# Gate stage of a PEER block: two-byte compares, scaling and copies swapped between engines, 64 early expert rows, and a new share of side work per step

## The chip, the cores and the metric

The kernel runs on one core of a Trainium2 chip. Its time is the device time of one execution in microseconds (us), the median of several. The engines are called PE (TensorE, matmuls), PEld (its weight loads), DVE (VectorE), ACT (ScalarE), POOL (GpSimd) and SP (SyncE, which here only issues DMAs). Every engine works through its own instructions in order.

## The reference, cut to what matters

Two transformer blocks over 512 tokens of width 1024, all in float32. The change lies in the first block, in the part called PEER: every token picks, for each of 8 heads, 16 experts out of 128 x 128, and adds their value vectors, weighted.

```python
q = (nf @ w_q).reshape(t, PEER_HEADS, D_KEY)
s1 = jnp.einsum("thd,hkd->thk", q1, sub_keys[:, 0])
s2 = jnp.einsum("thd,hkd->thk", q2, sub_keys[:, 1])
v1, i1 = lax.top_k(s1, TOPK)
v2, i2 = lax.top_k(s2, TOPK)
cand = (v1[..., :, None] + v2[..., None, :]).reshape(t, PEER_HEADS, TOPK * TOPK)
vals, ci = lax.top_k(cand, TOPK)
e1 = jnp.take_along_axis(i1, ci // TOPK, axis=-1)
e2 = jnp.take_along_axis(i2, ci % TOPK, axis=-1)
idx = (e1 * N_KEYS + e2).reshape(t, PEER_HEADS * TOPK)
gates = jax.nn.softmax(vals.astype(jnp.float32), axis=-1).astype(n.dtype)
# for each block of 128 tokens:
act = jax.nn.gelu(jnp.einsum("td,tkd->tk", xb, expert_u[ib])) * gb
out = jnp.einsum("tk,tkd->td", act, expert_v[ib])
```

After it the second block begins with a state space mixer, whose tables (powers of the transition, input and output maps) depend on weights alone.

## The kernel before, in words

Every weight arrives as a strip of 128 x 1024 numbers (`wr`, loaded by SP), is split in two halves whose sum it is (`wh` by ACT, line 148; `wl` by DVE or POOL, line 150), and is multiplied in three matmuls (lines 161 to 163). Two strips ahead are split, four ahead are loaded (`next_strip`).

Tokens 128 to 511 are done **densely**, for all experts: the scores of 128 groups of 128 experts (strips `exp_u`) are computed, multiplied by a table `gd` that holds each token's gate for each expert and zero elsewhere, and multiplied by the value strips (`exp_v`) into six PSUM banks `pv` (line 1143). Tokens 0 to 127 are done by **rows**: for each of 128 slots a gather (POOL, line 1009) brings the u and v vectors of the expert that each token picked; DVE forms the dot product (line 1012) and adds the weighted v vector (line 1043).

The work falls in three stretches. First come the 16 query strips, with the top-16 picks on DVE. Then the **gate stage** (`plan_gates`): PE works on the u strips of 64 expert groups, whose results go out to memory (`sd`), and beside it a list `bg` of background items is worked off. An item has a cost, and after each strip items are taken until the strip's share of the total cost is used (`run_bg`). The items are:

- the choice of experts for a block of 128 tokens (`plan_choice`): candidates, top 16, and per head a look-up `look(h)`, in which DVE compares (line 861), POOL multiplies (line 864) and DVE reduces two heads later (line 868); then `ints` turns numbers to integers, `trans` transposes them on PE and copies them with ACT to the tables `e1T`, `e2T`, `gT`.
- 48 fronts of 8 tokens: `front(i)` builds one-hot tables, `oh2` (line 917, all 8 tokens, float32), `oh1` (line 925, four tokens, bf16 out) and `gh`, the one-hot times the gate, with ACT from `oh1` for four tokens (line 929) and with DVE in one step for the other four (line 931); `mid(i)` multiplies them on PE into two PSUM tiles `pg` (line 941); `back(i)` copies these with ACT to `gb` (line 948), from which ACT issues stores to `gd`. The number table they are compared with, `iotaP` (in the tile `held`), lies in PSUM as float32.
- `EARLY` = 32 row dots, each with a gather of the u half alone: 12 among the second block's 16 fronts, 12 among the third's, 8 after all else (`TAIL`).

Then the **dense stage** (`dense`): 128 steps, each with 18 `pv` matmuls and, in 64 of them, the 24 matmuls of a u strip not done before. How much background follows each step is set by `rates`. The background list is the rows (a cost of 1.2 for a slot whose dot is already done, 2.4 for one that needs gather, dot, gate and add) with the state space prep (`ssm_prep`: about 20 chains on DVE, then 16 parts of small POOL products, a few PE products, and stores that ACT issues) spread between them in proportion to cost. SP loads, in order, strips, the saved scores `gs` and every fourth step a 768 KB piece `G` of `gd`, four steps ahead of its use.

Of the kernel before, what the change touches and what calls it, by code (L numbers as in the profile page):

```python
# [36 lines left out]
class K:  # L37
# [557 lines left out]
    EARLY = 32  # L595
# [6 lines left out]
    NV = 4  # L602
    CV = 4
# [40 lines left out]
    def peer(self):  # L644
# [16 lines left out]
        iotaP = self.bank("mmc", (P, P), "held")  # L661
# [10 lines left out]
        self.bg = [(0.1, lambda: nc.scalar.copy(iotaP, iota))] + bias  # L672
# [63 lines left out]
        for what, i in self.q_order()[2:]:  # L736
            if what == "q":
                self.lin(xq, p_q(i))
            else:
                self.lin(nr, p_s(i), w=TD)  # L740
                done += 1
            if (what, i) == ("q", 11):
                self.run_bg(1000)
                part = self.plan_choice(vals, idx, iotaP, st_["rc"])
                self.bg += part(1, 0)
                self.bg_rate, self.credit = sum(c for c, _ in self.bg) / 8, 0
# [7 lines left out]
        self.plan_gates(part, iota, iotaP, gd, early)  # L754
# [49 lines left out]
    def plan_choice(self, vals, idx, iota, rc):  # L804
# [5 lines left out]
        self.eT = e1T, e2T, gT = [loc((P, TD), tag=t) for t in ("e1T", "e2T", "gT")]  # L810
        state = {}

        def part(b, half):
# [4 lines left out]
            def cands():  # L818
                if not half:
                    d["c"], d["k"] = loc((P, 8, NCD), tag="cand"), loc((P, 8, NCD), tag="code")  # L820
                    d["v"] = loc((P, 8, 16), tag="cv")
                    d["i"] = loc((P, 8, 16), U16, tag="ci")
                    d["e"] = loc((P, 8, 16), tag="ee")
# [32 lines left out]
            sh = [P, 16, NCD]  # L856

            def look(h):
                if h < 4 * half + 4:
                    eq = loc((P, 16, NCD), tag="eq", bufs=1 + self.LG)  # L860
                    nc.vector.tensor_tensor(
                        eq, d["i"][:, h, :].unsqueeze(2).to_broadcast(sh), iota[:, 0:NCD].unsqueeze(1).to_broadcast(sh), ALU.is_equal
                    )
                    nc.gpsimd.tensor_tensor(eq, eq, d["k"][:, h, :].unsqueeze(1).to_broadcast(sh), ALU.mult)
                    d["eq", h] = eq
                h -= self.LG
                if h >= 4 * half:
                    nc.vector.tensor_reduce(d["e"][:, h, :], d["eq", h], AX.X, ALU.add)

            if half:  # L870
                items += [(0.3, soft)]
# [16 lines left out]
            def trans():  # L888
                pt = self.px_((P, 3, P), "pt")
                nc.tensor.transpose(pt[:, 0, :], d["ef"][:, 0, :], self.ident)  # L890
                nc.tensor.transpose(pt[:, 1, :], d["ef"][:, 1, :], self.ident)
                nc.tensor.transpose(pt[:, 2, :], d["g"].rearrange("p a b -> p (a b)"), self.ident)
                o = slice(b * P - P, b * P)
                for j, t in enumerate((e1T, e2T, gT)):
                    nc.scalar.copy(t[:, o], pt[:, j, :])

            return items + [(self.IC if b == 1 else 0.8, ints)] + ([(0.3, trans)] if b else [])
# [3 lines left out]
    def plan_gates(self, part, iota, iotaP, gd, step):  # L901
# [3 lines left out]
        A = HT - self.NV  # L905
# [7 lines left out]
        def front(i):  # L913
            t0 = i * HT
            sh = [P, HT, P]
            oh2 = self.loc((P, HT, P), tag="oh2", bufs=2)
            nc.vector.tensor_tensor(
                oh2, e2T[:, t0 : t0 + HT].unsqueeze(2).to_broadcast(sh), iotaP.unsqueeze(1).to_broadcast(sh), ALU.is_equal
            )
            gh = self.loc((P, HT, P), tag="gh", bufs=2)  # L920
            A = HT - self.NV
            if A:
                oh1 = self.loc((P, A, P), BF16, tag="oh1", bufs=2)
                sh1 = [P, A, P]
                nc.vector.tensor_tensor(oh1, e1T[:, t0 : t0 + A].unsqueeze(2).to_broadcast(sh1), iotaP.unsqueeze(1).to_broadcast(sh1), ALU.is_equal)
# [38 lines left out]
        turn = {0: part(1, 1), 1: nxt[1], 2: nxt[2]}  # L964
        turn = {b: (x, x.pop())[1] for b, x in turn.items()}
        bg = part(1, 1)[:-1] + nxt[1][:3] + [turn[0]]
        nxt[1] = nxt[1][3:]
# [3 lines left out]
        for b in range(1, NB):  # L971
# [7 lines left out]
            for j in range(k):  # L979
                i = b * k - k + j  # L980
                bg.append((self.FC, lambda i=i: front(i)))
                if i >= 1:
# [82 lines left out]
    def dense(self, nr, gd, sd, xd, step):  # L1065
# [15 lines left out]
        costs, at, to = sum(c for c, _ in items), 0.0, 0  # L1081
        for it in items:
            at += it[0]
# [8 lines left out]
        scale = total / sum(rates[:-4])  # L1092
        rates = [r * scale for r in rates]

        def load(e):
            if e >= P:
                return
            if e % GG == 0:
                t = self.loc((P, NC, GG, TC), tag="G", bufs=2)
                nc.sync.dma_start(t, gd[:, :, e : e + GG, :].rearrange("c p e t -> p c e t"))  # L1100
                G[e // GG] = t
            if e in ahead:
# [18 lines left out]
        def unit_u(e):  # L1121
            load(e + 4)
            if e in ahead:
# [5 lines left out]
        self.bg_rate = 0  # L1129
        for e in range(4):  # L1130
            load(e)
        for e in range(L):
            unit_u(e)
        for e in range(P):
# [92 lines left out]
    def ssm_prep(self):  # L1227
# [144 lines left out]
        def part(q):  # L1372
# [29 lines left out]
            def w2(r):  # L1402
# [3 lines left out]
                w, x = self.loc(sh2, tag=f"w2{r}"), self.loc(sh2, tag="w2x")  # L1406
# [5 lines left out]
            def wc(r):  # L1412
# [3 lines left out]
                w, x = self.loc(sh3, tag=f"wc{r}"), self.loc(sh3, tag="wcx")  # L1416
# [798 lines left out]
```

## Time and profile before

| | us |
|---|---|
| median of 3 executions (3007.21 to 3015.2) | 3007.63 |
| the profiled execution, its own time | 3011.37 |
| its span in the trace | 3009.6 |
| gate stage, from the start of the one-hot work to the last early strip | 349 to 697 |
| dense stage, `pv` matmuls | 711 to 1591 |

The profiled execution is 3.7 us above the median, and 1.8 us of its time lie outside the span. PE is busy for 2870.4 us. [...] To read the profile: for each stretch take PE's idle time and lost clock, which is all that a change beside PE can give back, and look which engine PE waited for.

### The profile page before, as it was taken

The numbers are of one execution on the slowest core, as the hardware profiler recorded it, in microseconds if no ns is written. First come the engines' busy times: TensorE is split into PE (matmuls) and PEld (weight loads), VectorE is DVE, ScalarE is ACT, GpSimd is POOL, SyncE is SP. The second block draws the span as 40 slices with busy tenths as digits, with TensorE's granted clock in tenths as the row PEclk, the third lists the DMA queues.
The fourth block names the chain that finished last, engine by engine and source line by source line (L and its number), as shares of the span: only waits on it lengthen the run. The fifth ranks groups of instructions, "written<-read, shape, count | busy, mean of one in ns | idle before, by whom it ended". The sixth has DMA issues, their size and how long they took to land. (4 is left out here: it accounts for less than half of the span.)

```text
span 3009.6 us, 39311 instructions
## 1 busy us (share of the span) xinstructions
PE 2870.4 (95%) x14286; PEld 2428.0 (81%) x14286; DVE 2168.8 (72%) x3783; ACT 1257.4 (42%) x2200; POOL 1111.8 (37%) x937
## 2 busy tenths in 40 slices
PE   8999999998999999999999989999999998999998
PEld 6787999998888788877877768888878766888886
DVE  7849888986889888888876764766566366566665
ACT  4443355664334333333335443333344355433333
POOL 3134776752268787788762311000011011100001
PEclk9999999999999999999999999999999999999999
DMA  4236446788889899988873653332332211233323
GB/s 143 63 108 144 162 160 223 248 298 286 281 300 344 305 335 332 328 311 325 323 253 134 173 184 91 92 93 89 100 110 84 64 53 53 89 101 98 98 71 98
DMA packets 237793, 537.92 MB, mean 179 GB/s; under 512 B 35802, under 2 KB 130410, under 8 KB 224928
## 3 DMA queue, kind: packets, MB, share of 16 engines
q1 hardware_dynamic: 172896, 346.84, 35.2%
q0 software_dynamic: 25232, 140.74, 13.2%
q10 hardware_dynamic: 39472, 47.84, 4.5%
q8 instruction: 113, 1.85, 0.3%
q14 instruction: 80, 0.66, 0.1%
HBM read 470.33 MB, written 65.01 MB: 178 GB/s over the span
## 5 line engine op out<-in xcount | busy, mean ns | idle before, releaser
L150 DVE TENSOR_TENSOR wl<-wr,wh 128x1024 fp32r<-128x1024 f32 (+2 forms) x445 | 539.2, 1222 | 501.6 <-ACT wh L148 498.0
L148 ACT ACTIVATE wh<-wr 128x1024 fp32r<-128x1024 f32 (+2 forms) x552 | 545.2, 995 | 430.8 <-PE mm L163 220.5
L161 PE MATMUL mm<-xn,wh 128*128 128x512 f32 x1296 | 515.5, 398 | 13.7 <-ACT xn L119 8.4
L162 PE MATMUL mm<-xn,wl 128*128 128x512 f32 x1296 | 509.4, 393 | 0.9 <-POOL wl L150 0.9
L163 PE MATMUL mm<-xn,wh 128*128 128x512 f32 x1296 | 509.5, 393 | 0.6 <-DVE xn L114 0.6
L226 POOL TENSOR_TENSOR accs<-accs,sq 128x512 f32<-128x512 f32 x56 | 86.2, 1539 | 1028.0 <-ACT sq L225 1023.7
L1143 PE MATMUL pv<-wh,A 128*128 128x512 f32 x1536 | 442.8, 402 | 23.3 <-ACT wh L148 15.9
L150 POOL TENSOR_TENSOR wl<-wr,wh 128x1024 fp32r<-128x1024 f32 x107 | 259.8, 2430 | 448.2 <-ACT wh L148 430.8
L1143 PEld LDWEIGHTS pv<-wh,A 128*128 128x128 f32 x1536 | 291.6, 192 | 89.9 <-ACT wh L148 19.5
L162 PE MATMUL mm<-n,wl 128*128 128x384 f32 x1024 | 345.9, 338 | 5.5 <-DVE wl L150 3.6
L163 PE MATMUL mm<-n,wh 128*128 128x384 f32 x1024 | 346.1, 338 | 5.3 <-DVE n L114 5.3
L161 PE MATMUL mm<-n,wh 128*128 128x384 f32 x1024 | 351.2, 343 | 0.0
L161 PEld LDWEIGHTS mm<-xn,wh 128*128 128x128 f32 x1296 | 246.7, 190 | 66.1 <-ACT xn L119 8.4
L163 PEld LDWEIGHTS mm<-xn,wh 128*128 128x128 f32 x1296 | 245.7, 190 | 54.0 <-DVE xn L114 1.8
L162 PEld LDWEIGHTS mm<-xn,wl 128*128 128x128 f32 x1296 | 246.2, 190 | 52.9 <-POOL wl L150 1.3
L1143 PE MATMUL pv<-wl,A 128*128 128x512 f32 x768 | 246.3, 402 | 17.1 <-DVE wl L150 16.9
L117 ACT ACTIVATE A<-ga 128x384 fp32r<-128x384 f32 x128 | 67.3, 526 | 330.8 <-DVE ga L1108 329.4
L162 PEld LDWEIGHTS mm<-n,wl 128*128 128x128 f32 x1024 | 194.7, 190 | 8.5 <-DVE wl L150 3.9
L163 PEld LDWEIGHTS mm<-n,wh 128*128 128x128 f32 x1024 | 194.3, 190 | 5.6 <-DVE n L114 5.6
L161 PEld LDWEIGHTS mm<-n,wh 128*128 128x128 f32 x1024 | 194.7, 190 | 3.5 <-issue 0.8
L1143 PEld LDWEIGHTS pv<-wl,A 128*128 128x128 f32 x768 | 145.6, 192 | 59.7 <-DVE wl L150 28.0
L1701 ACT ACTIVATE uc<-up,vec 128x512 f32<-128x512 f32 x88 | 71.8, 816 | 203.8 <-DVE up L1699 203.8
(421 smaller groups left out, 5284.8 us busy)
## 6 DMA issues: line engine op xcount, KB each, us to landing
wr<-in_exp_u SPq DMA_DIRECT2D x128, 512.0 KB
wr<-in_exp_v SPq DMA_DIRECT2D x128, 512.0 KB
wr<-in_w_up SPq DMA_DIRECT2D x88, 512.0 KB
gd<-gb ACTq DMA_DIRECT2D x48, 512.0 KB
G<-gd SPq DMA_DIRECT2D x32, 768.0 KB
wr<-in_w_dn SPq DMA_DIRECT2D x64, 320.0 KB
sd<-gs SPq DMA_DIRECT2D x64, 192.0 KB
gs<-sd SPq DMA_DIRECT2D x64, 192.0 KB
```

Source lines behind the costliest of these rows:

```text
L117: nc.scalar.activation(hi, src, AF.Copy)
L148: nc.scalar.activation(s.hi, s.raw, AF.Copy)
L150: eng.tensor_tensor(s.lo, s.raw, s.hi.bitcast(F32), ALU.subtract)
L161: t.matmul(ps, wh, xh, start=start, stop=False)
L162: t.matmul(ps, wl, xh, start=False, stop=False)
L163: t.matmul(ps, wh, xl, start=False, stop=stop)
L226: self.later(1, lambda: nc.gpsimd.tensor_tensor(acc, acc, sq, ALU.add))
L1143: nc.tensor.matmul(pv[2 * b + h], a[:, x, o], w[:, h * T : h * T + T], start=(e == 0 and i == 0 and w is s.hi), stop=last)
L1701: nc.scalar.activation(c, u, AF.Identity, scale=w(2), bias=cb[:, m : m + 1])
```

## The change

- **Compares.** Both look-up and `oh1` compares take two-byte numbers: a bf16 copy `iotaB` of the number table, put in the spare half of the PSUM tile `held`; `e1T` holds each number twice side by side in bf16, and the look-up's numbers are doubled by ACT (`twice`). The outputs are bf16; a look-up's product goes to a tile `ec` of its own.
- **Scaling and copies.** `oh1` covers all 8 tokens, ACT scales all 8, and the fused DVE step is gone. DVE copies both `pg` tiles.
- **Turn of a block.** The transposes on PE and the copies behind them are two items, put one front apart, and the other items end a front earlier.
- **Rows.** `EARLY` is 64: 28 dots among the second block's fronts, 28 among the third's, 8 last.
- **Dense stage.** Side work is spread by cost less 0.8, so 0.4 for a slot with its dot done and 1.6 for another; the first two steps take no background; `G` is loaded two steps ahead of use, behind a first strip; the fetch of `pT` for the stage behind moves three steps earlier, ahead of the reload of x.
- Two scratch tiles of the state space prep share one buffer on POOL.

```diff
-    EARLY = 32
+    EARLY = 64
...
-        iotaP = self.bank("mmc", (P, P), "held")
+        held = self.bank("mmc", (P, T), "held")
+        iotaP, iotaB = held[:, 0:P], held[:, P : P + P // 2].bitcast(BF16)
...
             def look(h):
                 if h < 4 * half + 4:
-                    eq = loc((P, 16, NCD), tag="eq", bufs=1 + self.LG)
+                    sh = [P, 16, NCD // 2, 2]
+                    eq = self.tmp((P, 16, NCD), BF16, tag="eq")
                     nc.vector.tensor_tensor(
-                        eq, d["i"][:, h, :].unsqueeze(2).to_broadcast(sh), iota[:, 0:NCD].unsqueeze(1).to_broadcast(sh), ALU.is_equal
+                        eq.rearrange("p k (a b) -> p k a b", b=2),
+                        d["i2"][:, h].unsqueeze(2).to_broadcast(sh),
+                        iota[:, 0:NCD].rearrange("p (a b) -> p a b", b=2).unsqueeze(1).to_broadcast(sh),
+                        ALU.is_equal,
                     )
...
+            oh1 = self.loc((P, HT, P), BF16, tag="oh1", bufs=2)
+            sh1 = [P, HT, P // 2, 2]
+            nc.vector.tensor_tensor(
+                oh1.rearrange("p t (a b) -> p t a b", b=2),
+                e1T[:, t0 : t0 + HT, :].unsqueeze(2).to_broadcast(sh1),
+                iotaB.rearrange("p (a b) -> p a b", b=2).unsqueeze(1).to_broadcast(sh1),
+                ALU.is_equal,
+            )
             for t in range(HT):
-                e1, g = e1T[:, t0 + t : t0 + t + 1], gT[:, t0 + t : t0 + t + 1]
-                if t < A:
-                    nc.scalar.activation(gh[:, t, :], oh1[:, t, :], AF.Copy, scale=g)
-                else:
-                    nc.vector.tensor_scalar(out=gh[:, t, :], in0=iotaP, scalar1=e1, scalar2=g, op0=ALU.is_equal, op1=ALU.mult)
+                nc.scalar.activation(gh[:, t, :], oh1[:, t, :], AF.Copy, scale=gT[:, t0 + t : t0 + t + 1])
...
-                copy = nc.scalar.copy if q or i % 4 < self.CV else nc.vector.tensor_copy
-                copy(gb[:, c % 2, :, o : o + 4], pg)
+                nc.vector.tensor_copy(gb[:, c % 2, :, o : o + 4], pg)
...
-                m = -(-len(more) // max(1, k - 1 - j))
+                m = -(-len(more) // max(1, k - 2 - j))
                 bg += more[:m]
                 more = more[m:]
-            if b in turn:
-                bg.append(turn[b])
+                if j == k - 2:
+                    bg += ends[:1]
+                if j == k - 1:
+                    bg += ends[1:]
...
-            at += it[0]
+            at += it[0] - 0.8
...
+        rates = [r * scale * (e > 1) for e, r in enumerate(rates)]
...
         def unit_u(e):
             load(e + 4)
+            gates(e + 2)
...
+            if e == P - 5:
+                self.ple_fetch(0)
             if e == P - 3:
                 self.run_bg(100000)
                 nc.scalar.dma_start(self.x, xd)
-            if e == P - 2:
-                self.ple_fetch(0)
```

DVE in the gate stage, one front among the third block's. Before, then with the change (lines of `oh2` are 917 and 945, of `oh1` 925 and 951, of the copies 974, of the row dots 1012 and 1042):

```order
L917 TENSOR_TENSOR oh_1004_5921<-e2T_2336,held_1479 128x1024
L925 TENSOR_TENSOR oh_1006_5924<-e1T_2335,held_1479 128x512
L931 TENSOR_SCALAR gh_5923<-held_1479,e1T_2335,gT_2337 128x128 x4
L1012 SCALAR_TENSOR_TENSOR x,first<-x,accs 128x1024
L917 TENSOR_TENSOR oh_1009_5948<-e2T_2336,held_1479 128x1024
```

```order
L945 TENSOR_TENSOR oh_1043_6007<-e2T_2343,held_1479 128x1024
L951 TENSOR_TENSOR oh_1045_6010<-e1T_2342,held_1479 128x1024
L974 COPY gb<-pg_5991 128x128x4
L974 COPY gb<-pg_5996 128x128x4
L1042 SCALAR_TENSOR_TENSOR x,first<-x,accs 128x1024 x2
L945 TENSOR_TENSOR oh_1053_6071<-e2T_2343,held_1479 128x1024
```

Four fused steps went, two copies came, the second compare has twice the elements, and there are two row dots for one.

POOL in the dense stage, at the first part of the state space prep: the two products `w` with their scratch, and the gathers between them, which bring u and v (128x2048) before and v alone (128x1024) now:

```order
L1408 TENSOR_TENSOR w_1365_8197<-s_1136_6678,bb_7965 128x256
L1409 TENSOR_TENSOR w2x_8198<-s_1136_6678,bb_7965 128x256
L1410 TENSOR_TENSOR w_1365_8197<-w_1365_8197,w2x_8198 128x256
L1009 DMA gx<-in_rows_uv,first 128x2048
L1462 TENSOR_TENSOR tn_8204<-s_1139_6681,s_1138_6680 128x2x64
```

```order
L1444 TENSOR_TENSOR w_1487_8832<-s_1175_6793,bb_8564 128x256
L1445 TENSOR_TENSOR wcx_8833<-s_1175_6793,bb_8564 128x256
L1446 TENSOR_TENSOR w_1487_8832<-w_1487_8832,wcx_8833 128x256
L1039 DMA x<-in_rows_uv,two 128x1024 x2
L1499 TENSOR_TENSOR tn_8903<-s_1178_6796,s_1177_6795 128x2x64
```

While slots whose dots are done go by, gathers stand closer together and prep items further apart.

SP where the dense stage begins (`G` is the gate table's piece, `wr` a strip, `gs` saved scores):

```order
L729 DMA sd<-gs_6654 128x384
L1100 DMA G_6686<-gd 128x12x128
L1104 DMA gs_6688<-sd 128x384
L1104 DMA gs_6690<-sd 128x384
L1100 DMA G_6692<-gd 128x12x128
L135 DMA wr_6698<-in_exp_u 128x1024
```

```order
L747 DMA sd<-gs_6769 128x384
L135 DMA wr_6801<-in_exp_u 128x1024
L1130 DMA G_6803<-gd 128x12x128
L1136 DMA gs_6805<-sd 128x384
L1136 DMA gs_6807<-sd 128x384
L1136 DMA gs_6838<-sd 128x384
L135 DMA wr_6844<-in_exp_v 128x1024
```

A strip now stands ahead of the first piece, and another ahead of the second.

## Rows read from the trace of the kernel before

**Rows 1.** The page: PE's busy time, share of the span, instructions

```profile
PE 2870.4 (95%) x14286; PEld 2428.0 (81%) x14286; DVE 2168.8 (72%) x3783; ACT 1257.4 (42%) x2200; POOL 1111.8 (37%) x937
```

**Rows 2.** Busy us (instructions) by stretch; last three: PE clock, DMA share, GB/s

```profile
349.00:475.00 126.00, 119.47 (x750) 118.19 (x749) 113.57 (x352) 68.00 (x136) 89.35 (x75) 0.99 0.51 172
475.00:587.00 112.00, 102.66 (x651) 100.94 (x650) 101.44 (x221) 60.09 (x131) 76.77 (x55) 0.95 0.71 247
587.00:697.00 110.00, 106.57 (x721) 105.78 (x720) 82.04 (x155) 68.17 (x157) 59.23 (x35) 1.00 0.85 300
697.00:720.00 23.00, 16.47 (x71) 15.12 (x71) 13.88 (x20) 7.14 (x11) 6.39 (x5) 0.85 1.06 375
720.00:861.00 141.00, 141.00 (x673) 123.75 (x673) 124.47 (x287) 55.90 (x75) 43.53 (x35) 0.99 0.75 261
861.00:1590.00 729.00, 691.57 (x3287) 587.59 (x3286) 609.39 (x657) 279.89 (x534) 559.42 (x537) 0.98 0.88 317
1590.00:1600.00 10.00, 5.43 (x29) 4.28 (x28) 5.17 (x8) 4.35 (x9) 0.00 (x0) 0.85 0.42 165
```

**Rows 3.** What PE waited for, 861 to 1590: us, times, longest

```profile
PE pv L1143 <- DVE wl L150: 16.9, 19, 3.7
PE pv L1143 <- ACT wh L148: 15.9, 6, 5.1
```

**Rows 4.** DVE's groups, 349 to 697: count, busy us, mean ns, idle before

```profile
L931 DVE TENSOR_SCALAR gh<-held,e1T,gT 128x128 f32<-128x128 f32 x192 | 65.3, 400 | 0.0
L917 DVE TENSOR_TENSOR oh<-e2T,held 128x1024 f32<-128x1024 f32 x48 | 58.2, 1212 | 20.7 <-PE pg L941 15.6 <-ACT e2T L895 5.0
L1012 DVE SCALAR_TENSOR_TENSOR x<-x,accs 128x1024 f32<-128x1024 f32 x28 | 44.7, 1602 | 7.4 <-DMA x<-in_rows_uv,two 7.4
L925 DVE TENSOR_TENSOR oh<-e1T,held 128x512 bf16<-128x512 f32 x48 | 32.5, 678 | 0.0
...
L861 DVE TENSOR_TENSOR eq<-ci,held 128x800 f32<-128x800 uint16 x28 | 26.8, 976 | 0.1
```

**Rows 5.** Timeline at the two seams: start, us, engine, line, instruction, idle before

```profile
698.22 1.22 DVE L1012 SCALAR_TENSOR_TENSOR x<-x,accs 128x1024 f32<-128x1024 f32 x1 [10.54 <-DMA x<-in_rows_uv,two]
...
713.81 1.06 ACT L148 ACTIVATE wh<-wr 128x1024 fp32r<-128x1024 f32 x1 [2.97 <-DMA wr<-in_exp_u]
...
1589.27 1.28 DVE L1155 COPY gx<-pv 128x512 f32<-128x512 f32 x2
...
1593.99 0.63 ACT L117 ACTIVATE ph<-pT 128x512 fp32r<-128x512 f32 x1 [2.54 <-DMA wr<-in_w_pg]
...
1597.60 0.69 PE L781 MATMUL pt<-ident,gx 128*128 128x128 f32 x2 [3.79 <-DVE x L785]
```

**Rows 6.** ACT's groups, 349 to 697

```profile
L929 ACT ACTIVATE gh<-oh,gT 128x128 f32<-128x128 bf16 x192 | 61.4, 391 | 125.9 <-DVE oh L925 112.2 <-PE pg L941 6.9 <-issue 6.8
...
L948 ACT COPY gb<-pg 128x512 f32<-128x512 f32 x96 | 50.3, 576 | 0.2 <-PE pg L941 0.2
```

**Rows 7.** DVE's groups in the dense stage, 720 to 1590

```profile
L1012 DVE SCALAR_TENSOR_TENSOR gx<-gx,accs 128x1024 f32<-128x1024 f32 x58 | 84.2, 1452 | 6.3 <-DMA gx<-in_rows_uv,first 6.3
...
L1108 DVE TENSOR_TENSOR ga<-mm,G 128x384 f32<-128x384 f32 x62 | 33.9, 547 | 0.6 <-ACT mm L1117 0.6
```

**Rows 8.** What PE waited for, 349 to 697

```profile
PE pg L941 <- ACT gb L948: 9.9, 8, 3.3
PE pt L890 <- ACT gb L948: 5.1, 2, 3.3
PE pt L890 <- DVE ef L886: 2.4, 1, 2.4
```

**Rows 9.** POOL's gathers, 349 to 697: count, busy, mean ns

```profile
L1009 POOL DMA_INDIRECT x<-in_rows_uv,two x32 | 34.9, 1090 | 6.0 <-issue 3.1 <-DVE oh L925 0.3 <-DVE oh L917 0.2
```

**Rows 10.** What ACT waited for, 861 to 1590

```profile
ACT first L1036 <- DMA m3d<-wc: 29.5, 7, 5.2
```

**Rows 11.** What SP waited for, 861 to 1590

```profile
SPq L1100 <- DVE ga L1108: 175.0, 24, 9.6
```

More of the change, by code (lines that the diff above doesn't have):

```diff
@@ L601 @@
     HT = 8
-    NV = 4
-    CV = 4
     TD = T - P
@@ L659, in peer @@
         nc.scalar.dma_start(iota, I["c_iota"])
-        iotaP = self.bank("mmc", (P, P), "held")
+        held = self.bank("mmc", (P, T), "held")
+        iotaP, iotaB = held[:, 0:P], held[:, P : P + P // 2].bitcast(BF16)
+        identB = self.loc((P, P), BF16, tag="identB")
+        nc.scalar.copy(identB, self.ident)
         self.mm_tags = self.BUT_C
@@ L670, in peer, with hold, turn, again @@
         loads()
-        self.bg = [(0.1, lambda: nc.scalar.copy(iotaP, iota))] + bias
+        turned = self.loc((P, P), BF16, tag="turned")
+        def hold():
+            nc.scalar.copy(iotaP, iota)
+            def turn():
+                pt = self.px_((P, P), "pt")
+                nc.tensor.transpose(pt, iota, self.ident)
+                self.later(1, lambda: again(pt))
+            def again(pt):
+                nc.scalar.copy(turned, pt)
+                self.later(1, lambda: nc.tensor.transpose(iotaB, turned, identB))
+            self.later(1, turn)
+        self.bg = [(0.1, hold)] + bias
         zero = self.loc((P, 112), tag="zero")
@@ L753, in peer @@
         early, step = self.first_block(nt)
-        self.plan_gates(part, iota, iotaP, gd, early)
+        self.plan_gates(part, iotaP, iotaB, gd, early)
         self.bg_rate, self.credit = sum(c for c, _ in self.bg) / (R - done - self.RB), 0
@@ L809, in plan_choice @@
         loc = lambda shape, dt=F32, tag="l", bufs=1: pk.tile(list(shape), dt, tag=tag, name=self.name(tag), bufs=bufs)
-        self.eT = e1T, e2T, gT = [loc((P, TD), tag=t) for t in ("e1T", "e2T", "gT")]
+        self.eT = e1T, e2T, gT = loc((P, TD, 2), BF16, tag="e1T"), loc((P, TD), tag="e2T"), loc((P, TD), tag="gT")
         state = {}
@@ L868, in look, with twice @@
                     nc.vector.tensor_reduce(d["e"][:, h, :], d["eq", h], AX.X, ALU.add)
+            def twice():
+                nc.scalar.copy(d["i2"][:, hs], d["i"][:, hs].unsqueeze(3).to_broadcast([P, 4, 16, 2]))
+            items += [(0.2, twice)]
             if half:
@@ L888, in trans, with slots, plan_gates @@
             def trans():
[L889 to L897, printed above, removed]
+                d["pt"] = pt = self.px_((P, 3, P), "pt")
+                for j, x in enumerate((d["ef"][:, 0, :], d["ef"][:, 1, :], d["g"].rearrange("p a b -> p (a b)"))):
+                    nc.tensor.transpose(pt[:, j, :], x, self.ident)
+            def slots():
+                pt, o = d["pt"], slice(b * P - P, b * P)
+                nc.scalar.copy(e2T[:, o], pt[:, 1, :])
+                nc.scalar.copy(e1T[:, o, :], pt[:, 0, :].unsqueeze(2).to_broadcast([P, P, 2]))
+                nc.scalar.copy(gT[:, o], pt[:, 2, :])
+            return items + [(self.IC if b == 1 else 0.8, ints)] + ([(0.3, trans), (0.3, slots)] if b else [])
         return part
-    def plan_gates(self, part, iota, iotaP, gd, step):
+    def plan_gates(self, part, iotaP, iotaB, gd, step):
         nc = self.nc
         HT, TD = self.HT, self.TD
-        A = HT - self.NV
         e1T, e2T, gT = self.eT
@@ L962, in plan_gates @@
         nxt = {1: choose(0) + choose(2), 2: choose(3), 3: []} if self.EARLY else {1: choose(2), 2: choose(3), 3: choose(0)}
[L964 to L967, printed above, removed]
+        turn = {b: x[-2:] for b, x in ((0, part(1, 1)), (1, nxt[1]), (2, nxt[2]))}
+        for b in (1, 2):
+            del nxt[b][-2:]
+        bg = part(1, 1)[:-2] + nxt[1][:2] + turn[0][:1] + nxt[1][2:4] + turn[0][1:]
+        nxt[1] = nxt[1][4:]
         rows = [(1.2, lambda i=i: step(i)) for i in range(self.EARLY)]
@@ L981, in plan_gates @@
                 bg.append((self.FC, lambda i=i: front(i)))
+                ends = turn.get(b, [])
                 if i >= 1:
@@ L1079, in dense @@
         self.bg = []
-        costs, at, to = sum(c for c, _ in items), 0.0, 0
+        costs, at, to = sum(c - 0.8 for c, _ in items), 0.0, 0
         for it in items:
-            at += it[0]
+            at += it[0] - 0.8
             n = round(np_ * at / costs)
@@ L1091, in dense, with gates @@
         rates = [1.0 if e + L in ahead or e + L >= P else slow for e in range(P)]
[L1092 to L1098, printed above, removed]
+        scale = total / sum(rates[2:-4])
+        rates = [r * scale * (e > 1) for e, r in enumerate(rates)]
+        def gates(e):
+            if e < P and e % GG == 0:
                 t = self.loc((P, NC, GG, TC), tag="G", bufs=2)
@@ L1101, in load @@
                 G[e // GG] = t
+        def load(e):
             if e in ahead:
@@ L1129, in dense @@
         self.bg_rate = 0
+        self.dma_to(self.at + 1 + self.LA_DMA)
+        gates(0)
         for e in range(4):
```

20 lines of the change are left out of this document (9 added, 11 removed).

## The prediction

> **What bounds the kernel now.** The order of reading is: the page for the engine that works most, the windows for where that engine stands still, the groups of instructions for who is nearly full there, then the waits. PE is busy 95% of the span [rows 1]. The change takes no matmul away that counts, so it can only return what PE loses, as idle time or by a lower granted clock. The windows [rows 2] say where that is. In the gate stage the three thirds lose 6.5, 9.3 and 3.4 us of idle time (window less PE's busy time), and by the clock about 1 us (0.99 of 119.5), 5 us (0.95 of 102.7) and nothing: 25 us of 348. The seam to the dense stage, 697 to 720, loses 6.5 us and 2.5 by the clock. From 720 to 861, the stretch of rows whose dots are done, PE loses nothing but 1.4 by the clock. From 861 to 1590 it loses 37.4 us and 14 by the clock (0.98 of 691.6): 51 us, or 7.0%. The last seam loses 4.6 and under 1.
>
> In the gate stage DVE is the next bound: 113.6 + 101.4 + 82.0 = 297 of 348 us, 85%, and 90% in its first two thirds [rows 2]. In the dense stage PE waits for halves of strips: 16.9 us for DVE's, and 15.9 for ACT's, where six waits reach 5.1 [rows 3]; DVE is at 84%, POOL at 77% there [rows 2].
>
> **The change, DVE in the gate stage.**
> - Row dots: 32 more at 1.602 us = +51.3 [rows 4]. That mean holds while POOL and DMA run beside; a dot after a long wait took 1.22 [rows 5]: bounds +39 and +51. I take the mean of this stretch.
> - Fused compare and scale: 192 go, -65.3 [rows 4].
> - Copies of `pg`: 96 come. The trace of before has the same form on DVE at the end of the dense stage, two copies of 128x512 out of PSUM in 1.28 us, 0.64 each [rows 5]: +61.4. Bounds: 0.576, ACT's price for these copies [rows 6], and 0.73, from the product with 384 elements [rows 7] by 512/384: +55 to +70.
> - Look-up compares: 28 of 800 elements at 0.976 [rows 4]. No compare of before has two-byte numbers on all sides. If two elements go in one pass, 400 passes cost 0.57, from 0.547 for 384 [rows 7]: 28 x -0.41 = -11.4. If not, 0. I take the half price: the opcode stays and both inputs and the output shrink.
> - `oh1`: 48, now 1024 elements. Today's 512 elements, four-byte in, cost 0.678; 1024 four-byte ones cost 1.212 [rows 4]. At the half price 1024 cost what 512 do, 0; at the full price 48 x 0.534 = +25.6. Below nothing: a compare and scale of 128 elements costs 0.400 with its overhead [rows 4], eight times the elements in two-byte form hardly less than 0.4, so -13 is the floor. I take 0, by the same choice.
>
> Sum: 51.3 - 65.3 + 61.4 - 11.4 = +36, so 333 of 348 us, 96%. At full price it is 370, more than the stage has.
>
> [...]
>
> **By thirds.** The background goes by cost per strip, so the added dots also move fronts. Counted in the order of instructions, fronts 1 to 16 go beside 18.9 strips before and 17.2 now, fronts 17 to 32 beside 17.0 and 18.4, the rest up to the last strip beside 16.5 and 18.0. By PE's pace of before (126, 112, 110 us) these are 115, 121 and 120 us. DVE then has, with 20 look-ups in the first third and 8 in the second: first 113.6 - 1.3 (copies less fused steps) - 8.1 = 104 (90%, as before); second 101.4 - 1.3 - 3.3 + 16 x 1.6 = 122 (101%); last 82.0 - 1.3 + 16 x 1.6 = 106 (89%). The first third loses its stalls at a block's turn, 5.1 + 2.4 us of `pt` waits [rows 8], since transposes and copies now stand a front apart: -5. They can't all go, for PE then waits for `pg`, 9.9 us today, now on DVE's copy. The second is over its length; no third of the stage had DVE above 91% [rows 2], so 122 us of work take between 122 and 134, I take 130: +9. The last gets +3 from what is pushed into it. Gate stage **+7**, bounds -5 (all 25 us of loss are not to be had while DVE is at 96%) and +34 (full price).
>
> What hides the rest: ACT gains 192 scalings at 0.391 (two fronts' halves more of what it has), gives 50.3 of copies [rows 6], and adds eight small doublings: 196 us of 348 [rows 2] become about 223, covered; but its scalings wait for DVE's `oh1` (112.2 us of such waits now [rows 6]), and `wh` splits queue behind them. POOL gains 32 gathers at 1.09 = +35 on 225 [rows 9, 2], covered; each waits for a slot that DVE's dot frees, and `wl` splits queue behind. DMA is at 0.71 and 0.85 in the last two thirds; 16 half rows of 512 KB in each, by 247 and 300 GB/s, are some 27 us of transfer each, so up to about 0.95 and 1.0 [rows 2].
>
> **Seams.** At 713.81 ACT waited 2.97 us for a strip [rows 5] that now is loaded ahead of the first `G`; of the 9 us lost there I take -4 (the added early dots end later, so the 10.54 us wait for a gather at 698 may stay [rows 5]). At the end PE stood 3.79 us behind ACT's wait of 2.54 for a DMA [rows 5]; the fetch of `pT` now goes out three steps earlier: -4 of 5.4. Both bounds 0.
>
> **Dense stage.** DVE loses 32 dots at 1.452 = -46 us of some 734 [rows 7, 2]; POOL's gathers stay in number. Slots with their dots done make 64 x 1.2 of 230 in cost, a third of the list, for a seventh before (38 of 269): the quiet stretch, which ended at 861, reaches to about 1010 (the cost of the first two steps moves behind). There PE loses almost nothing, as between 720 and 861 [rows 2]: 150 us x 7.0% = -10.5. The 580 us behind carry 40.5 us of loss; DVE has fewer dots beside prep, but the prep is denser, 0.8 of it in two thirds of the list, 1.2 times the rate, so POOL goes from 77% towards 84% (my estimate from its 559 us [rows 2]), and the 29.5 us that ACT waits to issue stores [rows 10] stay. I take a fifth, -8, bounds 0 and -20. SP no longer stands 175 us on the freeing of `G` [rows 11]; no engine waited for that, so nothing. Dense **-19**, bounds -2 and -32.
>
> **Sum.** +7 - 8 - 19 = -20 on the profiled 3011.4, so 2991; that execution is 3.7 above the median, so I forecast **2988**, and by the bounds of the parts 2960 to 3012.
>
> **Rivals.**
> - *Rows cost the gate stage more than they give back (slower).* Place: the middle third, already 101% full on DVE, where POOL, DMA and gathers slow each dot. It decides once a dot takes 1.9 us instead of 1.6: 28 x 0.3 = 8 more, 130 us of work for 121, with each late copy holding `pg` and so PE, whose clock falls behind each gap: middle +18, last +10, first 0. The dense stage returns only the quiet stretch less some POOL, -6; seams -4. +18: **3026**. For it: 101% and the DMA share. Against it: dots of 1.45 to 1.6 already under the same neighbours.
> - *Two-byte compares at full price (the change doesn't do what it says).* +37 us of DVE: first third 121 of 115, second 134 of 121: gate stage +32 in place of +7: **3013**. [...]
> - *The work moves, the loss stays.* The gate stage pays its +7, the quiet stretch gives 10, but ACT's stores and denser POOL products take it back later (-2 left), seams -6: about -1 to -5: **3003**, no change.
> - *More comes back.* The gate stage is not stretched, since DVE, once it has the work, can be fuller than 91%; the dense stage loses half its 51 us; seams -8: 0 - 26 - 8 = -34: **2974**, and to 2960 with the stalls gone.
>
> **How the numbers follow.** A measurement of this kernel tells about 0.3% (9 us) from no change, so faster is under 2998.6 and slower over 3016.7. Forecast 0.44, more comes back 0.14, loss stays 0.17, rows cost more 0.14, full price 0.11. Faster: most of the forecast's (0.40) and 0.14, with 0.02 of loss stays: 0.56; slower: 0.14 and half of full price with a little more: 0.21; same 0.23. The range, 2955 to 3028, reaches to the slower rival and leaves about 2 in 10 outside.
>
> **What would show it.** Means of the two compares near 0.57 and 0.68 (half price) or 0.98 and 1.21; copies near 0.64; dots in the gate stage below 1.7; the gate stage 340 to 360 us from first one-hot to last early strip, PE's waits for `pt` under 3 us, DVE over 93%; PE's loss from 861 to about 1010 near 0, and the waits for `wl` well under 16.9. Wrong would be: `pg` waits of over 20 us, quiet stretch not longer, or PE's loss from 1010 on no smaller than before.

## The result: slower by 1.4%, 65 us lost in the gate stage and 20 returned by the dense stage

The changed kernel takes 3052.4 us (median of 4, 3044.2 to 3053.2) against 3009.3 before: a ratio of 1.0136 (95% interval 1.0123 to 1.0148), 43 us slower, outside the range on record. Its profiled execution took 3053.2 us, its span 3051.4, 41.8 more than before's.

The windows of the changed kernel say where. Columns as in [rows 2], its PE clock the share of the full clock that PE was granted; first the gate stage up to the first `pv` matmul, then the dense stage in two parts, then the middle third, the last third and the rest of the gate stage:

```profile
349.00:777.00 428.00, 360.93 (x2149) 352.62 (x2149) 348.13 (x700) 209.62 (x527) 269.37 (x199) 0.92 0.70 243
...
777.00:1028.00 251.00, 250.16 (x1213) 219.67 (x1212) 206.89 (x374) 98.43 (x131) 97.88 (x83) 1.00 0.83 281
1028.00:1636.00 608.00, 579.96 (x2774) 494.88 (x2772) 488.18 (x511) 232.05 (x420) 487.95 (x489) 0.98 0.88 303
...
489.00:643.00 154.00, 125.41 (x718) 121.78 (x717) 132.14 (x228) 68.24 (x174) 103.43 (x72) 0.88 0.72 247
643.00:742.00 99.00, 89.79 (x576) 88.34 (x575) 79.01 (x117) 52.60 (x142) 62.23 (x42) 0.97 0.87 309
742.00:777.00 35.00, 25.28 (x134) 24.63 (x134) 22.68 (x30) 11.39 (x24) 16.80 (x12) 0.85 1.01 370
```

And the same of the kernel before, cut at the same fronts and at its first `pv` matmul:

```profile
349.00:711.50 362.50, 339.65 (x2166) 335.76 (x2165) 307.54 (x740) 199.62 (x426) 231.74 (x168) 0.97 0.70 242
711.50:1591.00 879.50, 839.10 (x3985) 716.15 (x3983) 737.79 (x949) 339.80 (x615) 602.95 (x571) 0.98 0.86 309
...
489.00:602.00 113.00, 105.26 (x670) 103.55 (x669) 104.12 (x228) 62.26 (x138) 77.65 (x55) 0.96 0.71 246
602.00:678.00 76.00, 76.00 (x523) 76.00 (x522) 60.81 (x114) 48.52 (x115) 40.01 (x23) 1.00 0.84 299
```

The gate stage takes 428 us for 362.5, **+65.5**; the dense stage 859 for 879.5, **-20.5**; what follows ends 3 us sooner (1418.6 us before, 1415.4 now). The first third is as long as before; the middle one goes from 113 to 154 us, the fronts of the last from 76 to 99. The new thing in those two is the dots. PE stands idle for 67 us of the stage (428 less 360.93) where it stood idle for 23, which makes 44 of the 65.5; the other 21 are as many matmuls, within a hundredth, at a granted clock of 0.92 for 0.97 (in the trace of before it was 0.50 from 700 to 705 us, after PE had been busy for 0.09 of the 3 us ahead). Yet DVE has 348 us of work in 428, 81%, where 96% was forecast: it is not fuller than before (85%), it is emptier.

DVE's groups in the gate stage of the changed kernel (columns as in [rows 4]), where they answer to [rows 4]:

```profile
L1042 DVE SCALAR_TENSOR_TENSOR x<-x,accs 128x1024 f32<-128x1024 f32 x64 | 100.0, 1572 | 45.1 <-DMA x<-in_rows_uv,two 45.0
L974 DVE COPY gb<-pg 128x512 f32<-128x512 f32 x96 | 61.2, 678 | 0.1
...
L951 DVE TENSOR_TENSOR oh<-e1T,held 128x1024 bf16<-128x1024 bf16 x48 | 32.5, 677 | 0.0
...
L879 DVE TENSOR_TENSOR eq<-ci,held 128x800 bf16<-128x800 uint16 x28 | 15.1, 561 | 4.8 <-ACT ci L894 4.8
```

Each price of the sum came out: copies 61.2 us (61.4 taken), dots 1.572 (1.602), compares 0.677 and 0.561 (0.678 and 0.57). The last column of the first row is what the sum lacked: DVE stood 45 us at dots whose gather had not landed.

Who waited, in the same stretch (us, times, longest):

```profile
ACT gh L958 <- DVE oh L951: 158.4, 39, 14.4
POOL wl L150 <- ACT wh L148: 110.1, 31, 9.3
DVE x L1042 <- DMA x<-in_rows_uv,two: 45.0, 18, 9.6
...
PE mm L162 <- POOL wl L150: 22.0, 14, 2.5
...
PE pg L968 <- DVE gb L974: 14.2, 8, 4.8
...
PE pt L918 <- DVE gb L974: 11.2, 2, 5.8
```

And the first three of these before, from 349 to 711:

```profile
ACT gh L929 <- DVE oh L925: 112.2, 40, 11.5
POOL wl L150 <- ACT wh L148: 104.6, 36, 7.6
DVE x L1012 <- DMA x<-in_rows_uv,two: 18.4, 4, 10.5
```

DVE's and ACT's waits grew; POOL's sum for `wh` hardly did (and it is 138.0 in e2 below, where no gather is left), so it proves nothing by itself. But in their order the three make a ring. The timeline of DVE, ACT and POOL in the last third (start, us, engine, line, instruction, idle before) shows one turn of it:

```profile
667.39 1.23 DVE L1042 SCALAR_TENSOR_TENSOR x<-x,accs 128x1024 f32<-128x1024 f32 x1 [2.26 <-DMA x<-in_rows_uv,two]
...
669.67 0.68 DVE L951 TENSOR_TENSOR oh<-e1T,held 128x1024 bf16<-128x1024 bf16 x1
...
682.03 1.23 DVE L1042 SCALAR_TENSOR_TENSOR x<-x,accs 128x1024 f32<-128x1024 f32 x1 [4.12 <-DMA x<-in_rows_uv,two]
```

```profile
670.45 2.45 ACT L958 ACTIVATE gh<-oh,gT 128x128 f32<-128x128 bf16 x8 [5.11 <-DVE oh L951]
672.80 1.04 ACT L148 ACTIVATE wh<-wr 128x1024 fp32r<-128x1024 f32 x1
```

```profile
673.92 2.36 POOL L150 TENSOR_TENSOR wl<-wr,wh 128x1024 fp32r<-128x1024 f32 x1 [7.58 <-ACT wh L148]
676.42 0.98 POOL L1039 DMA_INDIRECT x<-in_rows_uv,two  x1
```

A late gather holds a dot (667.39); behind the dot stands `oh1` (669.67); ACT waited 5.11 us for it with eight scalings, and behind them stands the split `wh` (672.80); POOL waited 7.58 us for that with `wl` (673.92), and behind `wl` stands the next gather, which goes out at 676.42 although its slot was free at about 668.6; so the dot that needs it waits 4.12 us at 682.03, and the ring starts again: the slot that this dot leaves is free at 683.3, its gather goes out at 691.07, and the dot that needs it waits 5.26 us at 697.86. In these timelines DVE, ACT and POOL each work in order, so each passes its delay on, 2.26, 5.11, 7.58 and 4.12 us in this turn. The first dot's own lateness had two parts: its gather was issued at 657.69, behind a `wl`, and took 9.7 us to arrive; that of the dot at 682.03 took 5.6 from its issue, so there the late issue is what cost.

### The profile page after: what moved, and what is told of

Its sections match the earlier page's. It is cut to its first block, busy times and chain, and to the rows that moved or that the text cites. A ratio compares the mean times of both kernels' runs of the same rounds, so it can differ in the third digit from the quotient of the medians.

```text
span 3051.4 us, 39376 instructions
## 1 busy us (share of the span) xinstructions
PE 2883.5 (94%) x14288; PEld 2443.9 (80%) x14288; DVE 2167.6 (71%) x3687; ACT 1258.9 (41%) x2242; POOL 1134.7 (37%) x969
## 5 line engine op out<-in xcount | busy, mean ns | idle before, releaser
L162 PE MATMUL mm<-n,wl 128*128 128x384 f32 x1024 | 353.3, 345 | 31.7 <-POOL wl L150 22.0
L161 PE MATMUL mm<-n,wh 128*128 128x384 f32 x1024 | 357.1, 349 | 3.7 <-ACT gs L746 3.7
L163 PE MATMUL mm<-n,wh 128*128 128x384 f32 x1024 | 351.6, 343 | 5.0 <-DVE n L114 5.0
L161 PEld LDWEIGHTS mm<-n,wh 128*128 128x128 f32 x1024 | 199.3, 195 | 7.9 <-ACT gs L746 4.6
L163 PEld LDWEIGHTS mm<-n,wh 128*128 128x128 f32 x1024 | 198.7, 194 | 5.3 <-DVE n L114 5.3
L958 ACT ACTIVATE gh<-oh,gT 128x128 f32<-128x128 bf16 x384 | 117.6, 389 | 183.9 <-DVE oh L951 158.4
```

The lines of the kernel that those rows point to most:

```text
L161: t.matmul(ps, wh, xh, start=start, stop=False)
L162: t.matmul(ps, wl, xh, start=False, stop=False)
L163: t.matmul(ps, wh, xl, start=False, stop=stop)
```

## The experiments

Times of the gate stage (349 us to the first `pv` matmul), of DVE in it, and of the dense stage, from the windows and waits of each run's trace (stage starts differ by some 3 us; at 349 the choice of experts begins, and the first one-hot compare starts at 371 to 377, not at 349 as the table of times before has it). e9, e10, e11 and e13 are one execution each, e3, e5, e6 and e7 two:

| kernel | total, median | gate stage | DVE busy | DVE's waits for gathers | dense stage |
|---|---|---|---|---|---|
| before | 3009.3 | 362.5 | 308 | 18 | 879.5 |
| changed | 3052.4 | 428 | 348 | 45 | 859 |
| e1, 32 rows | 3005.3 | 380 | 303 | 20 | 864 |
| e2, dots without gathers | 2999.6 | 375 | 328 | 0 | 859 |
| e3, gathers without dots | 2988.8 | 369 | 253 | 0 | 858 |
| e4, copies on ACT | 3050.8 | 429 | 290 | 86 | 859 |
| e5, quarter, 4 dots each | 3083.9 | 462 | 412 | 10 | 856 |
| e6, quarter, 15 ahead, 4 dots each | 3091.3 | 467 | 411 | 9 | 858 |
| e7, before with 64 rows | 3057.1 | 423.5 | 365 | 39 | 862 |
| e8, before with dense edits | 2989.6 | 363 | 308 | 18 | 862 |
| e9, sums, full gathers | 3028.1 | 405 | 322 | 46 | 857 |
| e10, sums, quarter | 3012.3 | 390 | 324 | 27 | 855 |
| e11, sums, quarter, 15 ahead | 3003.8 | 388 | 327 | 9 | 853 |
| e12, 32 rows, old scaling, copies | 2997.9 | 365 | 295 | 18 | 867 |
| e13, 3 slots | 3078.7 | 457 | 337 | 82 | 855 |
| e14, e8 with 16 rows | 3004.3 | 363 | 294 | 17 | 880 |
| e15, e8 with two-byte compares | 2993.1 | 360 | 293 | 18 | 869 |
| e16, e15 with 16 rows | 2995.3 | 352 | 263 | 17 | 877 |

**e1: 32 rows.**

```diff
-    EARLY = 64
+    EARLY = 32
```

> The changed kernel with 32 early rows instead of 64 (12 dots beside the second block's fronts, 12 beside the third's, 8 last); all else is the change's. In the changed kernel the gate stage (349 us to the first pv matmul) takes 428 us, 65 more than the 363 before, the dense stage 859, 20 less. Both theories of the added rows (load: DVE simply has too much work there; gathers: DVE stands 45 us on gathers that have not landed) expect the gate stage back at 345 to 365 us, the dense stage near 875 and a total of 2990 to 3010. The rival that copies, scaling or the turn of a block cost the time expects the gate stage to stay over 395 us and the total over 3035.

Ratio to before 0.9993 (0.998 to 1.0007). 48 of the 65 us hang on the second 32 rows; 380 is 15 above what either theory expected, which e12 takes up.

**e2: dots without gathers, e3: gathers without dots.**

```diff
...
-            if i + 3 < E:
-                gather(x[:, (i + 3) % 4, :], half, self.two[:, 0, i + 3 : i + 4])
-            dot(i, x[:, i % 4, :])
+            dot(i, x[:, i % 4, :], 0.0)
```

> The changed kernel, 64 early dots, without the 64 gathers of u halves: the dots read what lies in the slots, scaled by zero so that nothing overflows, so that the picked rows' part of the output is wrong. DVE's work stays, its 45 us of waits for gathers go, and POOL and the DMA queues lose the gathers. Theory gathers: the gate stage falls from 428 by 45 or more, to 370 to 385 us. Theory load: DVE's work alone (348 us of 428) sets the time in the middle third, which stays over 140 of its 154 us, and the gate stage falls by 15 at most, to 413 or more.

```diff
...
-            dot(i, x[:, i % 4, :])
```

> The changed kernel with the 64 gathers of u halves but without their dots (the sums are set to zero once, so the picked rows' part of the output is wrong). DVE loses 100 us of work in the gate stage, and nobody there waits for a gather. Theories gathers and load both expect 345 to 365 us of gate stage. The rival that the transfers themselves slow the strips (DMA at 0.9 to 1.0 of its time, POOL's queue longer) expects 395 or more.

Without gathers 375 us, without dots 369 (4 above what was expected). DVE's group of dots in e2, to set beside the row above:

```profile
L1042 DVE SCALAR_TENSOR_TENSOR x<-x,accs 128x1024 f32<-128x1024 f32 x64 | 89.3, 1420 | 0.0
```

So neither the added work (64 dots, 89 us) nor the added transfers cost much alone: 12 and 6 us over before (which has 32 dots with their gathers). It takes both, a dot that must wait in DVE's order.

**e4: copies on ACT.**

```diff
-                nc.vector.tensor_copy(gb[:, c % 2, :, o : o + 4], pg)
+                nc.scalar.copy(gb[:, c % 2, :, o : o + 4], pg)
```

> The changed kernel with the 96 copies of pg back on ACT. DVE loses 61 us of 348 in the gate stage, ACT gains 55. Theory load: the gate stage falls from 428 to 375 to 390 us. Theory gathers: DVE still waits for the gathers, and more of it shows, since dots come up earlier; ACT gets its copies behind scalings: 405 to 420. Total accordingly 3000 to 3015 or 3030 to 3045.

DVE had 58 us less to do and the stage was 1 us longer. The waits took up the room:

```profile
DVE x L1042 <- DMA x<-in_rows_uv,two: 86.1, 28, 11.0
PE pg L968 <- ACT gb L974: 45.8, 18, 8.8
```

By DVE's load alone the stage should have fallen to 375 to 390, and it did not; e2 speaks against load alone as well, with 328 us of work in a stage of 375. Neither theory had named 429, but the one of the gathers had said that DVE's waits would show more. That the copies went from one link of the ring to another, so that its way round stayed as long, fits this. It isn't shown: PE now waits 45.8 us for copies that come late on ACT, where it waited 14.2 for DVE's, and e4 can't tell the two apart.

**e5 and e6: quarter gathers, three and fifteen ahead.**

```diff
...
+        eighth = rows.rearrange("e (h d) -> (e h) d", h=8)
...
-                gather(x[:, (i + 3) % 4, :], half, self.two[:, 0, i + 3 : i + 4])
+                gather(xq[(i + NQ - 1) % NQ], eighth, self.two[:, 0, i + NQ - 1 : i + NQ])
...
-            dot(i, x[:, i % 4, :])
...
+            for _ in range(4):
+                u = xq[i % NQ]
+                nc.vector.scalar_tensor_tensor(out=u, in0=u, scalar=0.0, in1=nt[:, 0 : 2 * P], ...)
```

> The changed kernel with the 64 early gathers at a quarter of their bytes (256 numbers of each row for 1024), same count, same four slots, three ahead; each dot of 1024 elements becomes four of 256, so DVE's work stays about the same. The picked rows' part of the output is wrong. Without any gather the gate stage took 369 us, with them 428. Theory bytes (transfers are too long for the queues that share them): 370 to 380. Theory lead (a gather is issued too late ahead of its dot, because POOL, ACT and DVE wait on each other in their orders): waits for gathers stay at 25 us or more and the stage at 395 to 420. Theory count (64 more instructions in POOL's order hold the splits of strips): 405 or more, and the next kernel the same.

> As the kernel with quarter gathers, but sixteen slots of a quarter row in the same space, so that a gather goes out fifteen dots ahead instead of three. Theory lead: DVE's waits for gathers fall under 12 us and the gate stage to 368 to 380. Theory count: 405 or more. Theory bytes: as with three ahead, 370 to 380 in both.

Both missed by far, since the premise was wrong: four dots of 256 cost far more than one of 1024. In e5, over its whole gate stage:

```profile
L1058 DVE SCALAR_TENSOR_TENSOR x<-x,accs 128x256 f32<-128x256 f32 x256 | 169.0, 665 | 16.4 <-DMA x<-in_rows_uv,two 9.6
...
L1058 DVE DVE_READ_ACCUMULATOR x<-x,accs 128x1 f32 x256 | 20.9, 81 | 0.0
```

They decide nothing on gathers. But they do show what load costs: beside e10 below, which has the same gathers, e5 has 87 us more work on DVE (412 for 324) and a stage that is 72 us longer.

**e9, e10, e11: the same with plain sums.**

```diff
...
-            dot(i, x[:, i % 4, :])
...
+            nc.vector.tensor_reduce(self.r4, u, AX.X, ALU.add)
```

> The kernel with quarter gathers cut each dot into four, which cost DVE 84 us more than one dot; so this set takes the same 1024 elements with one plain sum per row (as the sums over look-ups, 0.98 us for 800 elements, so some 1.25 each, 80 us for 64 where the dots take 105). Full gathers, three ahead; the picked rows' part of the output is wrong. Here and in the next two the DVE work is the same 320 us or so, and only the gathers differ. With copies taken off DVE (290 us of work) the gate stage stayed at 429 and the waits for gathers rose to 86 us. Theories bytes and lead: gate stage 400 to 430, waits 55 to 75 us. Theory that DVE's own work sets the length: 365 to 375.

> As the sums with full gathers, but a quarter of each row (the sum reads it four times over), three ahead. Theory bytes (a transfer of 512 KB takes too long beside the others): waits under 15 us, gate stage 355 to 372. Theory lead or count: waits over 40 us, 395 or more.

> As the sums with quarter gathers, but fifteen ahead. Theory bytes: no shorter than with three ahead. Theory lead: 20 us or more below three ahead, waits under 12. Theory count: 395 or more in both.

Here DVE has the same work (322 to 328 us, as in e2). No theory had all three: e9's waits (46 us) were under the 55 named, e10's 27 and 390 lay between what bytes and lead expected, and e11's waits fell as lead had it (9 us), but not its stage. Cleanest is the last third, front 33 to front 48 (start to start of their `oh2`): 81.0 us without gathers (e2), 81.0 with quarter gathers fifteen ahead, 86.7 three ahead, 94.6 with full gathers (98.5 in the changed kernel, 76.4 before). So 64 more instructions on POOL cost nothing there; lead and bytes, which both make a gather late, cost 6 and 8 us of it. The 388 of e11 comes from its opening, where fifteen gathers and more stood ahead of a `wl`, and PE waited 10.0 us for it: its middle third took 136 us, e2's 123. And e9 against the changed kernel: the same waits (46 and 45 us), 27 us less work on DVE, 23 us less stage. Most of the 27 is in the rows themselves, 77.6 us for the dots' 100.0:

```profile
L1059 DVE TENSOR_REDUCE r<-x 128x4 f32<-128x1024 f32 x64 | 77.6, 1213 | 46.1 <-DMA x<-in_rows_uv,two 45.7
```

The dots' mean hides why. In the changed kernel 51 of the 64 took 1.20 to 1.26 us. The other thirteen took 1.46 to 4.66, and each of them ended 1.1 us after an elementwise product on POOL, a `wl` or a look-up's `ec`; the longest:

```profile
540.08 2.40 POOL L150 TENSOR_TENSOR wl<-wr,wh 128x1024 fp32r<-128x1024 f32 x1
540.51 4.66 DVE L1042 SCALAR_TENSOR_TENSOR x<-x,accs 128x1024 f32<-128x1024 f32 x1
542.44 1.64 POOL L886 TENSOR_TENSOR ec<-eq,code 128x800 f32<-128x800 bf16 x1
```

POOL is done at 544.08, the dot at 545.17. No sum of e9 took over 1.222. So, as an estimate from 64 dots at 1.21, some 22 us of what counts as DVE's work are dots held up beside POOL's products, for 11 in the kernel before and 18 in e1, which has no more dots than that: a second loss beside the waits for gathers, and one that the number of dots alone does not set. Why a dot is held so and a sum is not, no run shows.

**e13: one slot fewer.**

```diff
...
-            if i + 3 < E:
-                gather(x[:, (i + 3) % 4, :], half, self.two[:, 0, i + 3 : i + 4])
...
+            if i + 2 < E:
+                gather(x[:, (i + 2) % 3, :], half, self.two[:, 0, i + 2 : i + 3])
...
```

> The changed kernel with three slots for early gathers instead of four, so that a gather goes out two dots ahead instead of three; nothing else. Theory lead: DVE's waits for gathers rise from 45 us to 65 to 90, the gate stage from 428 to 440 to 465. Rival (the lead is as good as any, transfers alone set it): waits under 52 us, stage within 5 us of 428.

As the theory of the lead expected: 457 us, and

```profile
DVE x L1042 <- DMA x<-in_rows_uv,two: 81.7, 26, 9.5
```

A fifth slot, and with it a longer lead of the full gathers, wasn't tried.

**e7: the kernel before with 64 rows.**

```diff
-    EARLY = 32
+    EARLY = 64
...
```

> The kernel before with 64 early rows for 32, and the one shared scratch buffer without which it does not fit; no other part of the change. Theory of the gathers: DVE waits on gathers there too, the gate stage goes from 362.5 us to 400 to 425, the total to 3030 to 3050. Rival (the rows only hurt with the change's scaling, copies and block turns): the stage stays under 380 and the total at 2995 to 3012.

The rows alone (with the one shared scratch buffer that makes room for them) do it: ratio 1.016 (1.013 to 1.019), gate stage +61, the total 7 us above what was expected. Who PE waits for there is another, since copies are on ACT:

```profile
PE pg L941 <- ACT gb L948: 47.2, 22, 6.1
```

**e12: old scaling and copies with 32 rows.**

```diff
-    EARLY = 64
+    EARLY = 32
...
-            oh1 = self.loc((P, HT, P), BF16, tag="oh1", bufs=2)
...
+            oh1 = self.loc((P, A, P), BF16, tag="oh1", bufs=2)
...
+                if t < A:
+                    nc.scalar.activation(gh[:, t, :], oh1[:, t, :], AF.Copy, scale=g)
+                else:
+                    nc.vector.tensor_scalar(out=gh[:, t, :], in0=iotaP, scalar1=..., scalar2=g, op0=ALU.is_equal, op1=ALU.mult)
...
-                nc.vector.tensor_copy(gb[:, c % 2, :, o : o + 4], pg)
+                nc.scalar.copy(gb[:, c % 2, :, o : o + 4], pg)
```

> The changed kernel with 32 early rows, and with scaling and copies as before: oh1 for four tokens (two-byte), ACT scales those, the fused DVE step does the other four, ACT copies pg. Kept are the two-byte compares, the new turn of a block and the whole dense stage. With 32 rows and the change's scaling and copies the gate stage took 380 us, with everything old 362.5. Theory that all eight scalings behind one compare and copies in DVE's order lengthen the chain of a front: the stage is back at 352 to 364 and the total at 2978 to 2992. Rival that the turn of a block or the new weights cost it: 375 or more, total over 2998.

Gate stage 365 for 380: the change's scaling and copies together cost some 15 us at 32 rows, while DVE's work is 8 us apart. Total ratio 0.997 (0.9956 to 0.9985), a little over what was expected.

**e8: only the dense edits; e14: with 16 rows.**

```diff
-            at += it[0]
+            at += it[0] - 0.8
...
+        rates = [r * scale * (e > 1) for e, r in enumerate(rates)]
...
+            gates(e + 2)
...
+            if e == P - 5:
+                self.ple_fetch(0)
...
```

> The kernel before with only the dense stage's part of the change: side work spread by cost less 0.8, two first steps without background, the gate pieces behind a first strip and two steps ahead, the fetch of pT three steps earlier. 32 early rows and the old gate stage. In the changed kernel with 32 early rows the dense stage took 864 us against 879.5 before. If that came from these edits: gate stage 362, dense stage 862 to 867, total 2986 to 2993, better than both kernels. Rival (it is the other side of the longer gate stage, where the same strips' side work was done): dense stage 875 to 880, total 3000 to 3008.

```diff
-    EARLY = 32
+    EARLY = 16
```

> The kernel before with the dense edits (2990 us, dense stage 862 us, gate stage 363) and 16 early rows for 32. By the prediction's step (rows taken out of the dense stage shorten it, 19 us for 32) the dense stage would grow by 9 to 10 us and the total to about 2995. If the rows buy next to nothing there (859 with 64 rows, 862 with 32): dense stage 862 to 866, gate stage 356 to 361, total 2984 to 2990.

e8 is the fastest kernel that still does all the work (e3, without its dots, took 2988.8): 2989.6 us, ratio 0.9935 (0.9913 to 0.9957), 20 us under the kernel before. Its dense stage is 862 us with 32 rows. With 16 rows it is 880, while the gate stage stays (363): neither expectation named this, 17 us for 16 rows where the prediction's step gives 9 to 10. Rows do pay in the dense stage, up to a point. e7's, with 64 rows and no dense edit, is 862 as well. So either the edits or the second 32 rows bring 17 to 18 us, and both together only 20.5.

**e15 and e16: two-byte compares on top of e8, 32 and 16 rows.**

```diff
...
+                        d["i2"][:, h].unsqueeze(2).to_broadcast(sh),
...
+                e1T[:, t0 : t0 + A, :].unsqueeze(2).to_broadcast(sh1),
...
```

> The kernel before with the dense edits and the two-byte compares (look-ups, and oh1 for four tokens); 32 rows, scaling, copies and the turn of a block as before. The compares free DVE of 28 x 0.41 and 48 x 0.27 us, 25 in all, in a stage where DVE's work and its waits fill 90%. If that sets the length: gate stage 340 to 355, total 2970 to 2983. If PE's own work and the fronts' chain through PSUM set it: 358 to 364, total 2985 to 2992.

> The same with 16 early rows. With the rows' step of the prediction: 5 to 10 us slower than with 32. If rows buy nothing in the dense stage and cost gathers in the gate stage: as fast or up to 6 us faster than with 32.

The compares took 24.5 us less, as expected (26.8 to 15.1 for the look-ups, 32.6 to 19.8 for `oh1`), but DVE lost only 15 us of work by the windows, since the 32 dots went from 49.6 to 60.6 us: again dots that end 1.1 us after a product on POOL, the longest 8.06 us. The gate stage lost 3; the total, 2993.1 (ratio 0.9955, 0.9937 to 0.9973), is not below e8's. With 16 rows: gate stage 8 us shorter, dense stage 8 longer, no difference in the total.

## Why the prediction was wrong

- **The reading of what bounds the kernel** held: PE loses little, DVE is next in the gate stage.
- **DVE's sum** held: +36 was forecast for 349 to 697; over the whole stage DVE's work went from 307.5 to 348.1, +40.6. Its mean for a dot, 1.602 us, was right by the size but is no price of the operation: it has in it the dots held beside POOL (six of before's 32, 1.47 to 5.69 us). The half price of the two-byte compares was the author's estimate from [rows 4] and [rows 7], for a form that no run had shown yet; it held, 0.561 and 0.677 us for 0.57 and 0.678, with the table in PSUM. So the rival of compares at full price is out, and nothing of the 43 us is a compare.
- **The step that failed is "Gate stage +7"**. It let the new work go into time in which DVE stood idle, to 96% of the stage, and in its paragraph on what hides the rest the 32 gathers were called covered because POOL and DMA had time left over. But DVE's work and its waits for gathers went from 326 us (307.5 and 18.4) to 393 (348.1 and 45.0), +67, and the stage +65.5: what DVE spent on neither stayed as it was, 37 us before and 35 now (38 or 39 in e9, e10 and e13). e2 is the sum without its gathers, and it gave +12. A gather's price was not POOL's 1.09 us but the dot that stands waiting at the head of DVE's queue: 45 us of waits for 18. [rows 4] showed 7.4 us of such waits with 28 dots, and [rows 5] one of 10.54; I read the latter as a matter of the seam. POOL's 7.58 us behind ACT was visible in its kind as well, in ACT's 112.2 us of waits for `oh1` [rows 6].
- **The rival "rows cost the gate stage more"** had place and sign but not the mechanism: it wanted dots of 1.9 us, and they took 1.57 (that some of them are slowed beside POOL was right). It gave the stage +28 and it was +65.
- **The block's turn**: -5 was forecast; PE's waits for `pt` grew, 11.2 and 6.3 us for 5.1 and 2.4 [rows 8].
- **Dense stage -19**: measured -20.5. The quiet stretch ran from 777 to 1028 with PE busy 250.16 of 251 us, and for the 32 us behind them without a loss; the forecast's, from 711 to about 1010, was as long. But its cause was put down to rows alone, with nothing for the moved gate pieces and spread; e7 and e8 show that rows or those edits give nearly the same, each without the other. Which of the edits does it was not tried.
- **DMA**: by the rates that the prediction names, 16 half rows are 34 and 28 us of transfer, not 27 each; the shares that it draws from them, 0.95 and 1.0, are in order. Measured were 0.72 and 0.87, in thirds that had grown. Nothing else hung on it.
- **Seams**: the last gave 3 us of 4; the first gave nothing: PE still stood 6.11 and 3.61 us there, now for DVE's `wl` behind the last dots.

Open: how much of the ring would go with a longer lead of full gathers, how the 65 us divide between late gathers and dots held beside POOL (e9 puts 23 us on dots against sums, in a single execution), and how the 15 us of e1 over e12 divide between scaling and copies.

## What to carry to other kernels

A dot that waited here for its gather cost not its 1.22 us but its wait and what stood behind it: 45.0 us of DVE's waits in the changed kernel, 18.4 before, in a stage 65.5 us longer. Before more operations that wait for a transfer are put in, count how far ahead the transfer is issued (two dots ahead gave 82 us of waits in e13, three 45), and follow the issuing queue back: if it waits, over other engines, for the queue that waits for it, as POOL did here for ACT (7.58 us) and ACT for DVE (5.11), the waits feed themselves. DVE's share of busy time fell from 85% to 81% while the stage grew, because waits came on top of the load; the added work and added waits of this fullest engine, 41 and 27 us, make up the stage's 65. Work shifted to another engine of the ring gave nothing (e4, 429 us for 428), work taken out of it did (e9, 405). Look also at the spread of an operation's durations before its mean is taken for a price. Test an edit of many parts one part at a time: here the dense edits alone were worth 20 us, and the rows hid them.

## What the runs showed of the hardware

- A compare of two-byte numbers, table in PSUM, result two-byte: 0.677 us for 1024 elements, 0.412 for 512 (e12), 0.561 for 800, where the forms of before, with the table in four bytes, took 1.212, 0.678 and 0.976.
- A dot of 1024 elements with its sum took 1.22 us on the median (changed kernel and e2) and 0.08 for reading the sum; the means of 1.57 and 1.42 come from dots that lasted until 1.1 us after a product on POOL, up to 4.66 us (8.06 in e15). Sums of as many elements took 1.20 to 1.22, all 64 (e9).
- A dot of 256 took 0.425 us on the median and 0.665 on the mean, and again 0.081 for reading the sum (e5).
